# The second MLP's down projection: first products written by ScalarE, and the residual added by accumulating DMAs inside the stage

## The chip, the cores and the metric

The kernel runs on one core of one Trainium2 chip. It is one launch. The metric is the device time of that launch in microseconds (us), over several runs. All profile rows are of one profiled execution; times in them count from the start of its span.

The engines have short names. PE is the matrix engine (TensorE), PEld its weight loads, DVE the vector engine, ACT the scalar engine, POOL GpSimd. SP is the engine that issues nearly all DMAs here; "SPq" rows are those issues, and each of them only tells when the transfer was handed to the DMA engines, not when it landed.

## The reference, cut to what matters

The kernel computes one inference step of a two-layer encoder on 1056 rows, 1024 of a prompt and 32 of a sample, each of width 1024. Layer 0 is a matrix-memory mixer and an MLP, layer 1 a banded attention and an MLP. The change concerns layer 1's MLP:

```
u = x * (1 + sc2) + sh2
f = square(relu(u @ w_up[l])) @ w_down[l]
x = layer_norm(ALPHA * x + (1 + g2) * f, ln_g[l, 1], ln_b[l, 1])
```

w_up is 1024 x 4096 and w_down 4096 x 1024. g2 is a gate with one value per feature, and there are two sets of it: one for the prompt's rows, one for the sample's. The kernel works with the sum divided by ALPHA: x + gate * f, with gate = (1 + g2) / ALPHA. Everything is float32 in and out.

## The kernel before, in words

**Layout.** Activations lie with features on the 128 partitions: a tensor of width 1024 is 8 feature chunks (numbered fc) of 128 partitions x 1056 columns. The columns are cut into four quarters of 264 (QN); quarters 0 and 1 are column pair tp = 0, quarters 2 and 3 are tp = 1. The last quarter reaches from column 792 to 1055 and so holds both prompt and sample columns: whatever uses a gate there is two instructions, one of 232 columns and one of 32.

**Precision.** Each float32 operand is split in two parts: a high part, a cast by ACT (L89), and a low part, a subtraction by DVE (L90). A product is three matmuls: high x high, high x low, low x high. A weight is therefore of use to PE only when both ACT and DVE have handled it.

**Seven products.** Both projections of this MLP (function mlp7, L1140 and on) use a scheme with 7 products in place of 8 for a 2 x 2 block of blocks. The list PRODS (L1111) gives for each product the form of the weight, the form of the moving data, the PSUM bank it adds into, and the chunk and quarter of the result that take it. The products 0 and 2 share a bank, so do 3 and 5, and 4 and 6: the bank goes on accumulating, and it is read twice, once after each. So the second product of a bank can't start before the first reading of it has ended.

**The up stage.** PE computes 16 blocks of 256 hidden features (pb). Of each finished block, DVE and ACT make seven forms of the hidden values (h_forms: HL on L1189, HM on L1194), which SP stores to DRAM as hd. Blocks 14 and 15 are stored plainly (hpl, L1184).

**The down stage.** The hidden blocks 0 to 13 are worked off in five groups (GRP, L1108): group 0 has 2 blocks, groups 1 to 4 have 3 each. A unit is a group g and a number m from 0 to 3, the pair of feature chunks 2m and 2m + 1. For one unit PE runs the 7 products for both column pairs: 2 x 7 x 2 x 3 = 84 matmuls in group 0, 126 in the later ones (unit, L1437 and on; the matmul is on L1452). For each product the function L.add is called: in this kernel add_gated_at (L1077), in which DVE computes ACX = PSUM * gate + ACX in place (L1082). In each unit the product is added to one of four places, (chunk, quarter); products 0, 2, 3 and 6 are the first to reach their place, 1, 5 and 4 the second. Two PSUM banks of eight are to spare while one unit is at work. Unit (0, 0) is split by column pairs, tp = 1 first; the others take both pairs product by product.

**Order.** PE's order in the down stage is written out in the program (a manual schedule). The order on DVE, ACT, SP and POOL is made by the planner ahead of time, from its own estimate of when operands are ready; at run time each engine works in that order and waits only for the operands of the next instruction.

**The weights.** For each unit, forms (L1260 and on) loads two blocks of w_down (rdn_d, issued on L1265) into three raw buffers that are used in turn, and makes four tiles of weight forms (wf_d). The loads go out on SP, in the same queue as everything else.

**The moving data.** fill (L1426 and on) loads the hidden forms of the next products from hd into free buffers (fx, fx_e, fx_w; issued on L1133). In group 0 and at its end the data of group 1 are loaded.

**The residual.** ACX, the sums, is two tiles: chunks 0 to 3 and chunks 4 to 7. In the up stage the same memory holds transformed inputs (TF), so the residual x is stored to DRAM (xsp[2]) by the norm before, and comes back by reload (L2092): each call loads two chunks, 1056 KB, on SP (L2097), and makes the tile anew on the first of each half. Calls 0 and 1 stand in the up stage, once the transformed inputs of pair 1 are done with; call 2 at its end (up_end), call 3 at the first unit of the down stage. So the first add of each place finds the residual there.

After the five groups a plain block of the down projection follows (hpl, L118 to L120), and the norm and the output per row tile (norm_out), with which the kernel ends.

Layer 0's MLP runs through the same mlp7 without the seven products in its down stage (NW = 0), and reloads its residual there by the same calls.

Of the kernel before, what the change touches and what calls it, by code (L numbers as in the profile page):

```python
# [10 lines left out]
AF = mybir.ActivationFunctionType  # L11
ALU = mybir.AluOpType
# [21 lines left out]
def segs(t0, n):  # L34

    out = []
    if t0 < TP:
        m = min(t0 + n, TP) - t0
        out.append((0, m, 0))
        if m < n:  # L40
            out.append((m, n - m, 1))
    else:
        out.append((0, n, 1))
    return out
# [31 lines left out]
def trunk_kernel(ctx: ExitStack, tc: tile.TileContext, a, o):  # L76
    nc = tc.nc
# [62 lines left out]
    xsp = [dr.tile([P, KC, T], F32, name=f"xsp{l}") for l in range(4)]  # L140
# [26 lines left out]
    def ada_part(l, i):  # L167
        return ada[:, l * 48 + i * KC:l * 48 + (i + 1) * KC, :]
# [39 lines left out]
    tp = tpt("tp_c")  # L208
# [13 lines left out]
    tp = tpt("tp_p2")  # L222
# [694 lines left out]
    def make_layer(acc, pp, uo, cut=None):  # L917
# [159 lines left out]
        def add_gated_at(t0, n, ps, gate, fc):  # L1077

            for off, m, x in pieces(t0, n):
                for o, mm_, cnd in segs(t0 + off, m):  # L1080
                    xs = x[:, fc, o:o + mm_]
                    nc.vector.scalar_tensor_tensor(xs, ps[:, off + o:off + o + mm_], gate[:, fc, cnd:cnd + 1], xs,  # L1082
                                                   op0=ALU.mult, op1=ALU.add)

        def out_proj(groups, order, wsrc, mov, gate, after_tb, nm, width=None, after_pr=None):
            for gi, grp in enumerate(groups):
                ws = {pr: [wsrc(pr, half) for half in range(2)] for pr in grp}
                for ti in order:
                    n = TBS[ti][1]
                    nn = n if width is None else width[ti]  # L1090
                    for pr in grp:
                        for j in range(2):
                            ps = mm(f"op_{nm}_{2 * pr + j}_{ti}")
                            proj(ps[:, :nn], nn, ws[pr], j, lambda hl, k: mov(hl, k, ti))
                            add_gated(ti, ps, gate, 2 * pr + j)
                            flow.tick(n / 96)
                        if after_pr:
                            after_pr(ti, pr)
                    if gi == len(groups) - 1:
                        after_tb(ti)  # L1100

        return mm, norm, norm_out, out_proj, gain_shift, add_gated_at

    QN = T // 4
# [33 lines left out]
    def mlp7(L):  # L1140
# [5 lines left out]
        l, mm, NW = L.l, L.alloc, L.nw  # L1146
# [279 lines left out]
        def fill(g, into, most=99):  # L1426

            kg = GRP[g][1]
            while want and len(rooms.free) >= kg and most:
                most -= 1  # L1430
                if g >= len(GRP) - 3:
                    late = g == len(GRP) - 1 or g == len(GRP) - 2 and len(into) < 10
                    rooms.free.sort(key=lambda r: any(r[0] is t for t in f4s[:3]) == late)
                tp, f = want.pop(0)
                into[tp, f] = rooms.load(hd[g][tp][f], kg)

        def unit(g, m, phases, ws, step, after):  # L1437


            kg = GRP[g][1]  # L1440
            for tps in phases:
                ps = {}
                for i, (w, f, b, c, q) in enumerate(PRODS):
                    for tp in tps:
                        first = (tp, b) not in ps
                        if first:
                            ps[tp, b] = mm(f"dn{l}_{g}_{m}_{tp}_{b}")
                        p = ps[tp, b][:, :QN]
                        for k in range(kg):
                            t, s0 = fx[tp, f][k]  # L1450
                            for n_, (wl, xl) in enumerate(((0, 0), (0, 1), (1, 0))):
                                nc.tensor.matmul(p, ws[w][:, wl, k], t[:, s0, xl], start=first and k + n_ == 0,  # L1452
                                                 stop=k == kg - 1 and n_ == 2, skip_group_check=not first)
                        L.add((2 * tp + q) * QN, QN, p, L.gate, 2 * m + c)
                        after(tp, f)
                        flow.tick(QN * kg / 768)
                    if tps is phases[-1]:
                        step(i)
# [4 lines left out]
        def up_end():  # L1463
            if NW:
                for t in L.rooms(tp1):
                    rooms.add(t)
                fill(0, fx)
            L.reload(2 if NW else 1)
        lone = max(j for j, (_, tp) in enumerate(jobs) if tp == tp0)
        sevens = {}  # L1470
        first_h = [(c, hl) for c in range(4) for hl in range(2)]
# [1 line left out]
        with tc.manual_schedule(engines={mybir.EngineType.PE}):  # L1473
            for _, j, i in sorted((7 * j + 2 * i, j, i) for j in range(len(jobs)) for i in range(7)):
                n, tp = jobs[j]
                if i == 0:
                    sevens[j] = Seven(seq[n][0], tp, got[n])
                sevens[j].product(i, up_end if j == len(jobs) - 1 else None)
                if tp == seq[n][1][-1]:
                    advance(n, i)  # L1480
                if j == lone and i == 6 and NW:
                    rooms.add(ep.tile([P, KG, 2, QN], F32R, tag="e", name=f"fx_e{l}"))
                    for t in L.rooms(tp0):
                        rooms.add(t)
                if j > lone + 1:
                    if i in (2, 4, 6) and NW:
                        fill(0, fx, 1)
                    if i in (2, 5) and not NW and first_h:
                        h_load(0, *first_h.pop(0))
                    if i == 0 and NW and j < lone + 4:  # L1490
                        L.reload(j - lone - 2)
                    if i == 0 and not NW and j == lone + 5:
                        L.reload(0)
        nu = len(seq)
# [34 lines left out]
        with tc.manual_schedule(engines={mybir.EngineType.PE}):  # L1529
            for i, (g, m, phases) in enumerate(units):  # L1530
                more = g + 1 < len(GRP)
                if i == 0:
                    L.reload(3)
                if i == 0:
                    rooms.add(ring.tile([P, KG, 2, QN], F32R, tag="wc", name=f"fx_w{l}", bufs=6))
                    fill(0, fx)
                if m == 1 and more:
                    want += [(tp, f) for f in order_f for tp in L.pairs]
                if g and m == 2 and more:
                    fill(g + 1, nfx)  # L1540

                def after(tp, f):
                    if m == 3 and more:
                        rooms.free += fx[tp, f]
                        fill(g + 1, nfx)

                def step(j):
                    advance(nu + i, j)
                    if g == 0 and m in (1, 2):
                        fill(g + 1, nfx, 1)  # L1550
                unit(g, m, phases, got[nu + i], step, after)
                if m == 3:
                    assert not want
                    fx, nfx = nfx, {}
# [7 lines left out]
        for t0, n in L.blocks:  # L1562
            for fc in range(KC):
                ps = mm(f"dn{l}_{fc}_{t0}")
# [14 lines left out]
    acc = open_acc(acc_half0)  # L1579
# [1 line left out]
        acc_dma(xsp[0][:, :, t0:t0 + n], acc["all"].part(t0, n))  # L1581
    h_cm = tc.tile_pool(name="oapool", bufs=1, reuse_waits="tile")
    hp = h_cm.__enter__()
    mm, norm, _, out_proj, _, add_gated_at = make_layer(acc, bank, uap)
    combine(0, lng(0), lnb(0), ada_part(0, 4), ada_part(0, 3))
    norms = {}

# [35 lines left out]
    class L0:  # L1623
        wups = wup0
        l, nw, pace, alloc, add, gate = 0, 0, 480, mm, add_gated_at, ada_part(0, 5)
# [30 lines left out]
        def reload(m):  # L1656
            i = m // 2
            if m % 2 == 0:
                acc["all"].tiles[i] = acc_half0(i, "ACX")
            k = m % 2 * 2  # L1660
            nc.sync.dma_start(acc["all"].tiles[i][:, k:k + 2], xsp[3][:, 4 * i + k:4 * i + k + 2])
# [25 lines left out]
    for gi, grp in enumerate(((0, 1, 2), (3,))):  # L1687
        ws = {pr: [wblock(f"q{pr}_{half}", wq, 512 * half, 256 * pr) for half in range(2)] for pr in grp}
        for ti, (t0, n) in enumerate(TBS):
# [9 lines left out]
            for fc in [f for pr in grp for f in (2 * pr, 2 * pr + 1)]:  # L1699
                g, r = fc // 2, 2 * (fc % 2)  # L1700
                gp, e = g // 2, g % 2
                ps = mm(f"q_{fc}_{t0}")
                proj(ps[:, :n], n, ws[fc // 2], fc % 2, lambda hl, k: uap(hl, k, t0, n))
                for hd in range(2):
                    for off, m, cnd in segs(t0, n):
                        if cnd == 0:
                            dst = QOT[ti][:, e, gp, 0:m // 64, (r + hd) * 64:(r + hd + 1) * 64]
                            src = ps[64 * hd:64 * hd + 64, off:off + m].rearrange("p (c i) -> p c i", i=64)
# [312 lines left out]
    def acc_half(i, name):  # L2021
        return accp.tile([P, 4, T], F32, tag=f"acc{i}", name=f"{name}{i}")
# [13 lines left out]
    def u2ap(hl, k, t0, n):  # L2036
# [2 lines left out]
    open_u2(1)  # L2039
    psD_cm = tc.tile_pool(name="psD", bufs=1, space=PSUM, reuse_waits="tile")  # L2040
    psD = psD_cm.__enter__()
    mm, norm, norm_out, out_proj, gain_shift, add_gated_at = make_layer(
        acc, lambda name: psD.tile([P, 512], F32, tag="mm", name=name, bufs=8), u2ap, 2 * QN)

    def wo_get(pr, half):
# [25 lines left out]
    class L1:  # L2071
        wups = wup1
        l, nw, pace, alloc, add, gate = 1, 14, 64, mm, add_gated_at, ada_part(1, 5)
        blocks = [(0, 288), (288, 256), (544, 256), (800, 256)]
        pairs, quarters = (1, 0), (3, 2, 1, 0)
        first = FIRST
# [12 lines left out]
            t = accp.tile([P, 2, 2, KG, QN], F32R, tag=f"acc{i}", name=f"TF{i}")  # L2089
            return [[t[:, n, hl] for hl in range(2)] for n in range(2)]  # L2090

        def reload(m):  # L2092
            i = m // 2
            if m % 2 == 0:
                acc["all"].tiles[i] = acc_half(i, "ACX")
            k = m % 2 * 2
            nc.sync.dma_start(acc["all"].tiles[i][:, k:k + 2], xsp[2][:, 4 * i + k:4 * i + k + 2])  # L2097

        def rooms(pr):

# [66 lines left out]
```

## Time and profile before

| | us |
|---|---|
| Median of 3 runs | 2411.29 (2409.8 to 2412.41) |
| The profiled execution's own time | 2412.41 |
| Its span, first to last instruction | 2410.6 |
| PE busy in the span | 2342.7 (97%) |
| DVE busy | 1939.0 (80%) |
| ACT busy | 1206.0 (50%) |
| POOL busy | 168.1 (7%) |

How to read it. The span is cut by the profile in busy time per engine; "x" gives a number of instructions. A row of a timeline or a group gives line, engine, operation, and "out<-in" by the program's names. Behind a row, "[0.92 <-DVE ACX L1082]" means that the engine was idle for 0.92 us ahead of it, and that the instruction on DVE that wrote ACX on line 1082 ended this. The row of a group has its count, its total busy time, the mean of one in ns, and the idle time ahead of its instructions by what ended it. The mean granted clock of PE in this execution is 0.995.

A window's row gives busy time and instruction count of PE, PEld, DVE, ACT and POOL, then PE's granted clock as a share of full speed, the mean busy share of the 16 DMA engines (it is modelled and can pass 1), and the GB/s moved. Matmuls overlap, so in short stretches PE's busy time says less than the number of matmuls.

In the stretch that the change touches, the down stage of layer 1 starts around 2042 us, its five groups end near 2341 us, and the outputs end the kernel.

### The profile page before, as it was taken

What the parts mean: (1) busy time and instruction counts of PE and PEld (TensorE: products, weight loads), DVE (VectorE), ACT (ScalarE), POOL (GpSimd) and SP (SyncE); (2) the same over time, 40 slices, a digit from 0 to 9 for tenths busy, and PEclk for the clock granted to TensorE, in tenths of its full rate; (3) what the DMA queues carried; (4) which work ended last, traced back from release to release, by engine and by line L of the source; (5) the groups of instructions that cost most, each with busy time, mean ns of one, the idle gap of its engine ahead of it and who ended that gap; (6) DMA issues with size and microseconds to landing.
All of it is one profiled execution on the core that took longest, in us unless ns stands there. A gap on an engine that the chain in (4) does not pass through costs nothing. (4 is left out here: it accounts for less than half of the span.)

```text
span 2410.6 us, 44188 instructions
## 1 busy us (share of the span) xinstructions
PE 2342.7 (97%) x17180; PEld 2250.4 (93%) x17180; DVE 1939.0 (80%) x3903; ACT 1206.0 (50%) x2454; POOL 168.1 (7%) x320
## 2 busy tenths in 40 slices
PE   7999999999999999999999999999999999899997
PEld 4999999999999999999999987789999999899997
DVE  4888766778788789989888777756998889888778
ACT  4565557278666630101147467773776777222212
POOL 0111100000000000000000224420000000000003
PEclk9999999999999999999999999999999999999999
DMA  8343222526566896675512330051486779976642
GB/s 302 120 131 103 78 89 66 177 91 206 184 198 200 279 336 230 252 261 215 183 56 89 82 93 1 10 140 59 165 278 211 259 278 335 355 256 236 224 146 73
DMA packets 284277, 424.64 MB, mean 176 GB/s; under 512 B 15384, under 2 KB 205228, under 8 KB 278948
## 3 DMA queue, kind: packets, MB, share of 16 engines
q1 hardware_dynamic: 279860, 391.48, 48.3%
q10 hardware_dynamic: 4208, 30.35, 3.1%
q8 instruction: 135, 2.21, 0.4%
q14 instruction: 74, 0.61, 0.1%
HBM read 305.96 MB, written 118.17 MB: 176 GB/s over the span
## 5 line engine op out<-in xcount | busy, mean ns | idle before, releaser
L1082 DVE SCALAR_TENSOR_TENSOR ACX<-dn,ada,ACX 128x264 f32<-128x264 f32 (+6 forms) x664 | 281.8, 447 | 83.2 <-PE dn L1452 41.1
L1452 PE MATMUL dn<-fx,wf_d 128*128 128x264 f32 x2016 | 254.1, 285 | 6.8 <-DVE ACX L1082 3.5
L1452 PEld LDWEIGHTS dn<-fx,wf_d 128*128 128x128 f32 x2016 | 248.8, 188 | 9.0 <-DVE ACX L1082 3.0
L89 ACT CAST w_dn<-raw_dn 128x1024 fp32r<-128x1024 f32 x36 | 37.7, 1050 | 282.1 <-DVE aw L279 136.9
L118 PE MATMUL dn<-hs,w_dn 128*128 128x384 f32 (+2 forms) x512 | 161.2, 315 | 0.0
L119 PE MATMUL dn<-hs,w_dn 128*128 128x384 f32 (+2 forms) x512 | 161.0, 315 | 0.0
L120 PE MATMUL dn<-hs,w_dn 128*128 128x384 f32 (+2 forms) x512 | 156.4, 314 | 1.3 <-DVE w_dn L90 1.3
L1317 PE MATMUL up<-TF,wf_u 128*128 128x264 f32 x1056 | 143.2, 285 | 3.8 <-ACT H L1320 3.8
L1317 PE MATMUL up<-U,wf_u 128*128 128x264 f32 x1056 | 140.3, 285 | 1.7 <-ACT H L1320 1.2
L1317 PE MATMUL up<-u,wf_u 128*128 128x264 f32 x1056 | 139.7, 285 | 1.3 <-ACT wf_u L89 0.7
L279 DVE SCALAR_TENSOR_TENSOR aw<-radw,cs,aw 128x512 f32<-128x512 f32 x196 | 139.5, 743 | 1.1 <-DMA radw<-in_w_ada_dram 1.1
L1317 PEld LDWEIGHTS up<-TF,wf_u 128*128 128x128 f32 x1056 | 134.4, 189 | 4.8 <-ACT H L1320 4.6
L1317 PEld LDWEIGHTS up<-U,wf_u 128*128 128x128 f32 x1056 | 133.0, 188 | 3.0 <-ACT H L1320 1.6
L1317 PEld LDWEIGHTS up<-u,wf_u 128*128 128x128 f32 x1056 | 132.9, 188 | 1.9 <-ACT wf_u L89 0.9
L118 PE MATMUL dn<-U,w_dn 128*128 128x384 f32 (+2 forms) x416 | 129.4, 312 | 0.6 <-DVE ada L304 0.6
L119 PE MATMUL dn<-U,w_dn 128*128 128x384 f32 (+2 forms) x416 | 129.4, 312 | 0.0
L120 PE MATMUL dn<-U,w_dn 128*128 128x384 f32 (+2 forms) x416 | 125.9, 313 | 0.6 <-DVE w_dn L90 0.5
L1817 ACT ACTIVATE p<-p,mx 128x576 f32<-128x576 f32 (+9 forms) x132 | 86.6, 657 | 27.5 <-DVE mx L1814 25.2
L120 PEld LDWEIGHTS dn<-hs,w_dn 128*128 128x128 f32 x512 | 96.0, 188 | 2.0 <-DVE w_dn L90 1.8
L118 PEld LDWEIGHTS dn<-hs,w_dn 128*128 128x128 f32 x512 | 96.5, 189 | 0.1
L119 PEld LDWEIGHTS dn<-hs,w_dn 128*128 128x128 f32 x512 | 96.6, 189 | 0.0
L90 DVE TENSOR_TENSOR HL<-H,HL 128x1056 fp32r<-128x1056 f32 x64 | 80.3, 1254 | 20.0 <-ACT HL L89 19.9
(403 smaller groups left out, 7111.0 us busy)
## 6 DMA issues: line engine op xcount, KB each, us to landing
hpl<-HL SPq DMA_DIRECT2D x144, 264.0 KB
rdn_u<-in_w_up_dram SPq DMA_DIRECT2D x64, 512.0 KB
hd<-HL SPq DMA_DIRECT2D x28, 1056.0 KB
fx<-hd SPq DMA_DIRECT2D x50, 528.0 KB
radw<-in_w_ada_dram SPq DMA_DIRECT2D x24, 1024.0 KB
hd<-HM SPq DMA_DIRECT2D x28, 792.0 KB
raw_up<-in_w_up_dram SPq DMA_DIRECT2D x40, 512.0 KB
raw_dn<-in_w_down_dram SPq DMA_DIRECT2D x36, 512.0 KB
```

Of the source, the lines that this page charges most:

```text
L89: nc.scalar.copy(dst_h, src)
L90: (eng or nc.vector).tensor_sub(dst_l, src, dst_h.bitcast(F32))
L118: nc.tensor.matmul(ps, wh, mov(0, k), start=(k == 0), stop=False)
L119: nc.tensor.matmul(ps, wh, mov(1, k), start=False, stop=False)
L120: nc.tensor.matmul(ps, wl, mov(0, k), start=False, stop=(k == nk - 1))
L279: nc.vector.scalar_tensor_tensor(acc[cnd], raw[:, k], sc, acc[cnd], op0=ALU.mult, op1=ALU.add)
L1082: nc.vector.scalar_tensor_tensor(xs, ps[:, off + o:off + o + mm_], gate[:, fc, cnd:cnd + 1], xs, op0=ALU.mult, op1=ALU.add)
L1317: nc.tensor.matmul(p, self.ws[w][:, wl, k], moving(f, tp, xl, k), start=first and k + n_ == 0, stop=k == 3 and n_ == 2, skip_group_check=n ...
L1452: nc.tensor.matmul(p, ws[w][:, wl, k], t[:, s0, xl], start=first and k + n_ == 0, stop=k == kg - 1 and n_ == 2, skip_group_check=not first)
L1817: nc.scalar.activation(z, z, AF.Exp, bias=mx[:, 0:1], scale=-1.0, accum_out=mx[:, 1:2])
```

## The change

1. The reloads of layer 1 are gone. Only the tiles are made anew, by fresh, which issues nothing: half 0 after the up stage's work for pair 1 is done, half 1 at the end of the up stage.
2. In group 0 the products 0, 2, 3 and 6, the first to reach their place, call L.put in place of L.add. There ACT writes PSUM * gate into ACX, and reads no residual. The other three products add to that on DVE as before.
3. The residual is added by eight DMAs with an accumulate operation, one per chunk (528 KB), from xsp[2] in DRAM onto ACX. They are issued from POOL's queue. In the program's order they stand ahead of these units: (1, 1) for chunks 4 and 5, (1, 2) for chunks 6 and 7, (2, 1) for chunks 0 and 1, (2, 2) for chunks 2 and 3. A unit (g, m) adds to chunks 2m and 2m + 1.
4. Layer 0 keeps its reloads as they were.

The diff, cut to its core:

```diff
+        def put_gated_at(t0, n, ps, gate, fc):
+            for off, m, x in pieces(t0, n):
+                for o, mm_, cnd in segs(t0 + off, m):
+                    nc.scalar.activation(x[:, fc, o:o + mm_], ps[:, off + o:off + o + mm_], AF.Copy,
+                                         scale=gate[:, fc, cnd:cnd + 1])
+
+        def add_stored(fc, src):
+            nc.gpsimd.dma_start(acc["all"].tiles[fc // 4][:, fc % 4], src[:, fc], accum_op=ALU.add)
...
-                        L.add((2 * tp + q) * QN, QN, p, L.gate, 2 * m + c)
+                        put = L.put if g == 0 and i in (0, 2, 3, 6) else L.add
+                        put((2 * tp + q) * QN, QN, p, L.gate, 2 * m + c)
...
-            L.reload(2 if NW else 1)
+                L.fresh(1)
+            else:
+                L.reload(1)
...
-                    if i == 0 and NW and j < lone + 4:
-                        L.reload(j - lone - 2)
+                    if i == 0 and NW and j == lone + 2:
+                        L.fresh(0)
...
-                if i == 0:
-                    L.reload(3)
...
+                for m_ in {(1, 1): (2,), (1, 2): (3,), (2, 1): (0,), (2, 2): (1,)}.get((g, m), ()):
+                    for fc in (2 * m_, 2 * m_ + 1):
+                        L.stored(fc, xsp[2])
                 unit(g, m, phases, got[nu + i], step, after)
...
+        put, stored = put_gated_at, add_stored
...
-        def reload(m):
-            i = m // 2
-            if m % 2 == 0:
-                acc["all"].tiles[i] = acc_half(i, "ACX")
-            k = m % 2 * 2
-            nc.sync.dma_start(acc["all"].tiles[i][:, k:k + 2], xsp[2][:, 4 * i + k:4 * i + k + 2])
+        def fresh(i):
+            acc["all"].tiles[i] = acc_half(i, "ACX")
```

More of the change, by code (lines that the diff above doesn't have):

```diff
@@ L1100, in out_proj @@
                         after_tb(ti)
-        return mm, norm, norm_out, out_proj, gain_shift, add_gated_at
+        return mm, norm, norm_out, out_proj, gain_shift, add_gated_at, put_gated_at, add_stored
     QN = T // 4
@@ L1583, in trunk_kernel @@
     hp = h_cm.__enter__()
-    mm, norm, _, out_proj, _, add_gated_at = make_layer(acc, bank, uap)
+    mm, norm, _, out_proj, _, add_gated_at, _, _ = make_layer(acc, bank, uap)
     combine(0, lng(0), lnb(0), ada_part(0, 4), ada_part(0, 3))
@@ L2041, in trunk_kernel @@
     psD = psD_cm.__enter__()
-    mm, norm, norm_out, out_proj, gain_shift, add_gated_at = make_layer(
+    mm, norm, norm_out, out_proj, gain_shift, add_gated_at, put_gated_at, add_stored = make_layer(
         acc, lambda name: psD.tile([P, 512], F32, tag="mm", name=name, bufs=8), u2ap, 2 * QN)
```

## The prediction, made before the changed kernel ran

> **What bounds the kernel now.** I read the page first, then the chain of waits, then windows cut at the units of the second MLP's down projection, then the timelines of PE, of SP's DMA queue and of ACT there.
>
> The page:
>
> ```profile
> span 2410.6 us, 44188 instructions
> PE 2342.7 (97%) x17180; PEld 2250.4 (93%) x17180; DVE 1939.0 (80%) x3903; ACT 1206.0 (50%) x2454; POOL 168.1 (7%) x320
> ```
>
> PE is the bound of the whole, so the change can only give or take PE's idle time. The chain, in order of time (start, us, engine, tile, line), shows where that is:
>
> ```profile
> 1819.92 201.48 PE up L1317 x1656
> ...
> 2094.09 0.56 DVE wf_d L90
> 2094.70 4.40 PE dn L1452 x34
> 2099.10 0.73 issue
> 2099.83 241.67 PE dn L1452 x1980
> ```
>
> From 2099.83 the chain is PE alone for 241.67 us. Whatever the change does, if it only acts around group 0, can be read from the time of that row: it is my marker, and its shift goes to the end unchanged. The windows show how much there is to win:
>
> ```profile
> core 0: us, PE busy (x) PEld busy (x) DVE busy (x) ACT busy (x) POOL busy (x), PEclk, DMA share, GB/s
> 2042.50:2058.50 16.00, 13.34 (x98) 12.08 (x97) 15.36 (x37) 7.99 (x15) 0.00 (x0) 1.00 0.99 340
> 2058.50:2069.10 10.60, 10.43 (x87) 10.22 (x85) 7.91 (x21) 0.41 (x1) 0.00 (x0) 1.00 1.03 400
> 2069.10:2082.30 13.20, 11.08 (x85) 10.50 (x86) 12.76 (x37) 4.99 (x13) 0.00 (x0) 1.00 0.98 364
> 2082.30:2094.70 12.40, 10.92 (x89) 10.49 (x87) 9.42 (x24) 1.03 (x2) 0.00 (x0) 1.00 1.04 411
> ...
> 2172.00:2203.00 31.00, 31.00 (x257) 31.00 (x256) 25.62 (x61) 6.60 (x14) 0.00 (x0) 1.00 0.39 139
> ```
>
> Undisturbed (last row), 257 matmuls take 31.00 us, 0.121 us each. The first four windows are the four units of group 0 (m = 0 to 3, 84 matmuls each, 10.2 us at that pace). They take 16.0, 10.6, 13.2 and 12.4 us, with the DMA engines full (0.98 to 1.04). Later, PE has no gap. The same place on PE (start, us, tile; behind it the idle time and what ended it):
>
> ```profile
> 2057.72 0.97 PE L1452 MATMUL dn<-fx,wf_d 128*128 128x264 f32 x6 [0.75 <-DMA fx<-hd]
> 2058.53 0.89 PE L1452 MATMUL dn<-fx_e,wf_d 128*128 128x264 f32 x6
> ...
> 2073.70 4.62 PE L1452 MATMUL dn<-fx,wf_d 128*128 128x264 f32 x36 [0.92 <-DVE ACX L1082]
> 2079.28 3.16 PE L1452 MATMUL dn<-fx,wf_d 128*128 128x264 f32 x24 [0.96 <-DVE ACX L1082]
> 2082.28 0.89 PE L1452 MATMUL dn<-fx_e,wf_d 128*128 128x264 f32 x6
> ...
> 2089.22 4.66 PE L1452 MATMUL dn<-fx,wf_d 128*128 128x264 f32 x36 [0.68 <-DVE wf_d L90]
> ```
>
> fx_e heads a unit, so units 1 and 3 start at 2058.53 and 2082.28 (unit 2 at the window's edge, 2069.1). Unit 0 ends when its last fx has landed (2057.72), which is issued ahead of the reloads that go: 2058.53 stays. From there three units of 10.2 us and the first 36 matmuls of group 1 (4.4 us) would bring the marker to 2093.5 instead of 2099.83. **At most 6.3 us can be won**, 0.26%. (About 0.2%, 4.8 us, is what a measurement of this kernel can tell from no change.)
>
> **The change, part by part.**
>
> *The evictions.* What writes ACX from the start of group 0 to its end (the reloads on SP among it), and ACT's nearest operations, the copy out of PSUM and an activation with two scale and bias vectors:
>
> ```profile
> L1082 DVE SCALAR_TENSOR_TENSOR ACX<-dn,ada,ACX x72: 240/486/495, 2045.2 to 2093.7; 128x264 f32<-128x264 f32 x40, 128x232 f32<-128x232 f32 x16, 128x32 f32<-128x32 f32 x16
> L2097 SPq DMA_DIRECT2D ACX<-xsp x2: 550/644/739, 2050.1 to 2058.7; - x2
> ```
> ```profile
> L1320 ACT COPY H<-up 128x264 f32<-128x264 f32 x132 | 49.0, 371 | 13.5 <-PE up L1317 13.3
> ...
> L935 ACT ACTIVATE u<-ACC,comb 128x256 fp32r<-128x256 f32 x8 | 4.7, 591 | 2.3 <-DVE ACC L992 2.3
> ```
>
> Products 0, 2, 3 and 6 of four units and two column pairs go to ACT. Where a product reaches into the sample's columns it is two instructions, so 10 of a unit's 18 go, 40 of the 72. DVE loses about 40 x 0.43 = 17 us of this stretch (0.43 is the mean over 24 full ones, 8 of 232 columns and 8 of 32; the row spans 0.24 to 0.49). A put costs between 0.37 and 0.59 us; I take 0.45, near the copy, since it has one vector: 40 x 0.45 = 18 us on ACT, 4.5 a unit, beside at most 5.0 us that ACT has in units 1 to 3. That is hidden. What it buys on PE is the two waits for adds in unit 2 (0.92, 0.96), the wait at 2089.22 (0.68; the weights' subtraction stood in DVE's queue between adds) and, of the start of group 1, the time that the subtraction at 2094.09 stood behind adds. Together some 3.5 us, if nothing else is late.
>
> *The reloads.* SP's queue (start, us, line, tile) and the casts of weights on ACT that answer to it:
>
> ```profile
> 2063.57 8.02 SPq L1265 DMA_DIRECT2D rdn_d<-in_w_down_dram  x2
> ...
> 2080.75 2.35 SPq L1265 DMA_DIRECT2D rdn_d<-in_w_down_dram  x2
> ```
> ```profile
> 2068.63 0.41 ACT L89 CAST wf_d<-rdn_d 128x256 fp32r<-128x256 f32 x1 [11.49 <-DMA rdn_d<-in_w_down_dram]
> ...
> 2092.53 0.51 ACT L89 CAST wf_d<-rdn_d 128x384 fp32r<-128x384 f32 x1 [0.50 <-DMA rdn_d<-in_w_down_dram]
> ```
> ```profile
> L2097 SPq DMA_DIRECT2D ACX<-xsp x4: 550/670/992, 1977.4 to 2058.7; - x4
> ```
> ```profile
> ACX<-xsp SPq DMA_DIRECT2D x8, 1056.0 KB
> ```
> ```profile
> 2045.00:2105.00 60.00, 52.84 (x407) 50.19 (x407) 51.61 (x132) 15.31 (x34) 0.00 (x0) 1.00 1.00 376
> ```
>
> The weights that SP asks for at 2080.75 are those of group 1's first unit, and the cast at 2092.53, ended by their landing some 10 us later, is **the gate**: PE gets them at 2094.70. The full DMA queue sets it. All four reloads are issued from 1977.4 to 2058.7, 1056 KB each; the two at 2050.1 and 2058.7 stand in front of the gate: 2 x 1056 KB at 376 GB/s is 5.75 us of a queue that is never empty. Without them the first cast of unit 2 (2068.63) comes about 5 us earlier, before unit 1 ends, so what unit 2 waits for at 2069.1 goes too. Of the 5.75 us up to 1.7 can be lost where SP stands 8.02 us for a free buffer (2063.57) while the queue drains. So the gate would be at 2086.8 to 2088.5. The two earlier ones I cost at nothing: the chain's first row is PE alone from 1819.92 on for 201.48 us, with no wait for a DMA; if that cover were gone it would be a gain of at most as much again. SP's own issue time (0.6 us each) hides nothing now.
>
> *The accumulating DMAs.* In the program they stand ahead of units of groups 1 and 2, but POOL has nothing else here (0.00 in every window). Each is held back by its operands alone, and nothing is queued behind it. So for rows 4 and 5 they start when unit 2's adds are done, by my count at about 2079 and not at 2111; for rows 6 and 7 after unit 3, at about 2089; for rows 0 to 3 after the first two units of group 2, near 2173 and 2188, where the DMA share is 0.39 and nothing suffers. The adds that wait for them come three units (46 us) later, so no wait on DVE.
>
> The first pair falls into the full queue, ahead of the gate. Its bytes are one reload's, 1056 KB, 2.9 us of the DMA engines if an accumulate costs what a load does. No row shows an accumulate, nor how two queues share full engines. Below: it takes only what is left over, the gate stays at 2086.8. Above: it goes first at two or three times the price, 8.6 us and more. I take the load's price, the nearest row, and equal turns: it starts at 2080 to 2081 and has all of its 2.9 us before the gate's data land, so the gate is at 2089.7 to 2091.4, middle 2090.6.
>
> The Trainium skill, "DMA: Bandwidth & Descriptors", section "Queues, rings and completion order", says that an engine takes turns between queues packet by packet, which is the equal turns taken here; no run shows it yet.
>
> *The sum.* The gate moves from 2092.53 to 2090.6: -1.9 us. Behind the gate PE now starts 2.2 us later; with DVE freed (0.51 for the cast, 0.55 for the subtraction) 1.3 us, so -0.9 more. The second pair, in the queue from 2089, takes another 2.9 us from the inputs of group 1's first unit and the next weights; their slack behind the gate covers most of it, and I charge 1.1. Sum: -1.9 - 0.9 + 1.1 = **-1.7 us**. Of the 6.3 us the gate and the second pair keep 4.6. The profiled execution took 2412.41 us, 1.8 over its span, and the median of the runs is 2411.29; laid on the median this gives **2409.6**.
>
> **The rivals.**
>
> *The accumulates don't touch the gate* (they start later than I say, held until the whole half of the sums is written, or they get only idle engines). For it: a wait by whole tiles would put all four behind unit 3. Against it: the queue has no idle time until 2105. Gate at 2086.8 to 2088.5, PE gets through group 0 without waits, marker at 2093.5 to 2095: -5.5 us, 2405.8.
>
> *An accumulate costs twice a load.* It reads its destination as well as its source. Pair one has 5.75 us to take, but by turns no more than the queue itself moves from 2081 to the gate's data, 3.5 to 5 us: gate at about 2092.0. -0.5 there, -0.9 from DVE, and pair two at twice its 1.1: +0.8, 2412.1. The Trainium skill, "Collectives: The Full Stack", section "The bandwidth ceiling: the fold count and why AG ≠ RS ≠ AR", gives two source reads as the reason why an adding transfer runs at about half the rate of a copy.
>
> *The accumulates slow the queue all through group 1's first unit* (the side of slower). The queue, full until 2105 in the window above, comes some 5 us earlier without the reloads, so from 2081 on it has about 16 us of work left for that unit (my estimate: what stood in it from 2086 to 2102). Equal turns with both pairs all that time make it 32. Against the 16 more stand the 5 us of the earlier start and about 5 us by which the last inputs land ahead of their use: +6, 2417.3. It decides when the four take over 16 us of the engines, that is 2.8 times a load's price.
>
> *The puts stand behind casts that wait for weights* (ACT's queue is in order). At 2068.63 ACT waited 11.49 us for a DMA; a put behind such a cast keeps a PSUM bank and so the fifth product. In unit 3 this would add the rest of the unit, 36 matmuls, behind the gate instead of ahead of it: +2.7 on the sum, 2412.3. Against it: DVE's adds, under the same planner, mostly stand ahead of the weights' work.
>
> *The change does nothing* (the adds were hidden and the DMA bytes only move by 30 us): within the first two cases, 0.
>
> **How the numbers follow.** Forecast 0.36, double price 0.22, no touch on the gate 0.22, slow queue 0.14, puts behind casts 0.06. Faster by over 0.2% is the third, and a little of the forecast where the gate comes early: 0.24. Slower by over 0.2% is the slow queue and a little of the last: 0.16. Within: 0.60. The likeliest case gives 2409.6, with its own bounds -4.5 to +1. The range runs from the full 6.3 us won (2405.0) to +4.2 (2415.5); outside it lies most of the slow queue and little else.
>
> **What would show it.** In the profile after: the put lines on ACT x40 at about 0.45 us; 40 fewer adds on DVE in group 0; SP without L2097's rows; unit 2 without waits for adds; the cast behind group 1's first weights at about 2090.6; POOL's DMA issues near 2079, 2089, 2173 and 2188; the long PE row starting near 2098. I am wrong if the gate comes before 2088 or after 2094, if the issues come only at their place in the program, if PE waits for a put, or if a gap opens on PE after group 1's first unit.

## The result, and the profile after

The changed kernel took **2419.01 us** in the median of 6 runs (2417.5 to 2420.32), the kernel before 2410.55 in 6 runs beside it (2406.25 to 2412.81): ratio 1.0038, 95% interval 1.0025 to 1.005. It is slower, by some 8 us, and outside the range. The profiled execution took 2418.34 us. Of its page, the span, the engines and two DMA queues (packets, MB, share of 16 engines' span):

```profile
span 2416.6 us, 44207 instructions
...
PE 2342.4 (97%) x17180; PEld 2250.9 (93%) x17180; DVE 1920.2 (79%) x3863; ACT 1221.6 (51%) x2494; POOL 175.1 (7%) x328
...
q1 hardware_dynamic: 279284, 387.15, 47.8%
...
q0 software_dynamic: 1152, 4.33, 0.9%
```

PE is busy as long as before (2342.7), so the page shows the loss as idle time; the rows below put some 2 us of it down to a lower clock. DVE has the 40 fewer instructions, ACT the 40 more. q0 is POOL's queue, and its 4.33 MB are the eight accumulates. They cost 0.9/4.33 of the engines per MB, q1's transfers 47.8/387.15: 1.7 times as much.

The chain of waits (start, us, what) no longer ends in one row of PE from the start of group 1 on:

```profile
2115.87 50.71 PE dn L1463 x414
...
2170.03 9.88 DMA rdn_d<-in_w_down_dram
...
2181.03 5.87 PE dn L1463 x45
...
2188.09 9.35 DMA rdn_d<-in_w_down_dram
2198.50 0.93 DVE wf_d L90 x2
...
2200.10 147.03 PE dn L1463 x1188
```

PE alone from 2115.87, then twice a load of weights that takes almost 10 us, both in group 2, where the prediction had no wait at all. PE's timeline there (idle time and what ended it in brackets), and DVE's rows for the first difference that it forms from new weights:

```profile
2167.14 1.63 PE L1463 MATMUL dn<-fx_w,wf_d 128*128 128x264 f32 x12
...
2181.03 4.39 PE L1463 MATMUL dn<-fx,wf_d 128*128 128x264 f32 x33 [2.38 <-DVE ACX L1082]
2185.25 1.63 PE L1463 MATMUL dn<-fx_w,wf_d 128*128 128x264 f32 x12
...
2200.10 7.26 PE L1463 MATMUL dn<-fx,wf_d 128*128 128x264 f32 x42 [4.45 <-DVE ACX L1082]
2207.21 1.62 PE L1463 MATMUL dn<-fx_w,wf_d 128*128 128x264 f32 x12
```
```profile
2180.01 0.56 DVE L1292 TENSOR_TENSOR s_d<-rdn_d,rdn_d 128x384 f32<-128x384 f32 x1 [4.67 <-DMA rdn_d<-in_w_down_dram]
...
2197.53 0.56 DVE L1292 TENSOR_TENSOR s_d<-rdn_d,rdn_d 128x384 f32<-128x384 f32 x1 [6.85 <-DMA rdn_d<-in_w_down_dram]
```

In the kernel before, the first of these (L1281 there) had no wait and the second had 0.80 us:

```profile
2179.03 0.55 DVE L1281 TENSOR_TENSOR s_d<-rdn_d,rdn_d 128x384 f32<-128x384 f32 x1
...
2192.52 0.56 DVE L1281 TENSOR_TENSOR s_d<-rdn_d,rdn_d 128x384 f32<-128x384 f32 x1 [0.80 <-DMA rdn_d<-in_w_down_dram]
```

PE waits for adds (L1082), because DVE, whose order is fixed, stands at L1292 in front of those adds until weights land. The issues on POOL and on SP say what met there:

```profile
...
2085.46 0.86 POOL L1094 DMA_DIRECT2D ACX<-xsp  x1 [7.92 <-DVE ACX L1082]
2088.27 0.89 POOL L1094 DMA_DIRECT2D ACX<-xsp  x1 [1.95 <-ACT ACX L1089]
2167.46 0.88 POOL L1094 DMA_DIRECT2D ACX<-xsp  x1 [78.30 <-DVE ACX L1082]
2169.89 0.86 POOL L1094 DMA_DIRECT2D ACX<-xsp  x1 [1.56 <-DVE ACX L1082]
2186.44 0.86 POOL L1094 DMA_DIRECT2D ACX<-xsp  x1 [15.69 <-DVE ACX L1082]
2187.82 0.88 POOL L1094 DMA_DIRECT2D ACX<-xsp  x1 [0.52 <-DVE ACX L1082]
```
```profile
2167.80 0.38 SPq L1276 DMA_DIRECT2D rdn_d<-in_w_down_dram  x1
...
2170.03 0.38 SPq L1276 DMA_DIRECT2D rdn_d<-in_w_down_dram  x1
...
2186.58 1.89 SPq L1276 DMA_DIRECT2D rdn_d<-in_w_down_dram  x2
```

The end of a unit releases both: its last adds set the accumulates free, and its last weight forms set the raw weight buffers free. So accumulates are issued at 2167.46 and 2169.89 and weights at 2167.80 and 2170.03, and again all four within some 2 us from 2186.44 on. The windows behind the second meeting (columns as in the prediction):

```profile
2190.00:2195.00 5.00, 5.00 (x43) 5.00 (x42) 0.49 (x1) 0.93 (x2) 0.00 (x0) 1.00 1.04 220
2195.00:2200.00 5.00, 0.65 (x6) 0.44 (x4) 2.46 (x7) 0.92 (x2) 0.00 (x0) 0.76 0.37 95
2200.00:2205.00 5.00, 4.90 (x24) 4.93 (x25) 4.64 (x12) 0.00 (x0) 0.00 (x0) 0.56 0.00 0
```

The DMA engines are full (1.04) and move 220 GB/s, where they moved 340 to 411 in the full windows of before; DVE works 0.49 of 5 us. After PE's gap the granted clock is 0.76 and then 0.56, so PE's 42 matmuls take 7.26 us instead of 5.08 (0.121 each).

**Where the time went.** In PE's timeline there is one fx_w row in each of the eight units of groups 1 and 2, the next one in the first unit of group 4, and an exu row late in the up stage, where both kernels are still alike. From these rows follow the lengths of nine pieces, and each less the same of before is a loss that doesn't depend on what came earlier in the execution. Before they are, from 2008.10 (exu) and 2104.30 (the first fx_w) on, 96.20, 15.37, 15.41, 15.35, 20.48, 15.36, 15.36, 15.36 and 65.81 us. The first piece holds the end of up and group 0; the next three steps lie in group 1, the one from 4 to 5 reaches into group 2, the next three lie there, and the last piece covers group 3.

| kernel | to 1st fx_w | 1 to 2 | 2 to 3 | 3 to 4 | 4 to 5 | 5 to 6 | 6 to 7 | 7 to 8 | 8 to 9 | sum |
|---|---|---|---|---|---|---|---|---|---|---|
| the change | -3.43 | 2.88 | 0.03 | 0.00 | 0.00 | 2.75 | 6.60 | 0.01 | 0.04 | +8.88 |
| no accumulates | -2.26 | 0.00 | 0.02 | 0.28 | 0.07 | 0.00 | 0.00 | 0.00 | 0.00 | -1.89 |
| chunks 4 to 7 only | -3.20 | 2.87 | 0.01 | 0.00 | 0.00 | 0.00 | 0.00 | 0.00 | 0.00 | -0.32 |
| chunks 0 to 3 only | -4.98 | 0.00 | 0.00 | 0.00 | 0.00 | 2.99 | 6.17 | 0.01 | 0.01 | +4.20 |
| plain loads | -2.94 | 0.00 | 0.00 | 0.00 | 0.02 | 0.00 | 1.85 | 0.00 | 0.00 | -1.07 |
| quarters | -4.12 | 2.14 | 0.00 | 0.25 | 0.07 | 0.00 | 0.53 | 0.01 | 0.00 | -1.12 |
| one chunk to a unit | -4.29 | 0.00 | 2.25 | 2.88 | 0.07 | 0.89 | 4.32 | 0.01 | 4.19 | +10.32 |
| the same in quarters | -3.06 | -0.01 | 0.18 | 0.63 | 0.08 | 0.00 | 0.55 | 0.00 | 1.06 | -0.57 |
| copies, two chunks | -3.03 | -0.01 | 0.00 | 5.25 | 2.39 | 5.56 | 6.33 | -0.01 | -0.07 | +16.41 |
| copies, one chunk | -5.07 | -0.01 | 2.39 | 2.20 | 0.05 | 1.31 | 6.15 | -0.02 | 2.08 | +9.08 |
| held, two chunks | -4.57 | -0.01 | 0.01 | 0.51 | 0.05 | 9.61 | -0.01 | -0.01 | -0.08 | +5.50 |
| held, one chunk | -3.81 | -0.01 | 0.22 | 0.24 | 0.06 | 1.86 | -0.01 | -0.02 | 1.84 | +0.37 |
| held, apart | -4.46 | 0.00 | 0.00 | 0.23 | 0.06 | 1.50 | 1.00 | -0.01 | -0.07 | -1.75 |

The first row sums to +8.88, beside +8.46 between the medians: 0.55 won around group 0 and its end (the first two columns, below called the seam), 9.35 lost in group 2. The other rows belong to the experiments below; each is one profiled execution, so a first column may differ by a microsecond or two by chance.

### The profile page after: what moved, and what is told of

Same layout as the page of the kernel before. It is cut to its first block, busy times and chain, and to the rows that moved or that the text cites. A ratio compares the mean times of both kernels' runs of the same rounds, so it can differ in the third digit from the quotient of the medians.

```text
span 2416.6 us, 44207 instructions
## 1 busy us (share of the span) xinstructions
PE 2342.4 (97%) x17180; PEld 2250.9 (93%) x17180; DVE 1920.2 (79%) x3863; ACT 1221.6 (51%) x2494; POOL 175.1 (7%) x328
## 3 DMA queue, kind: packets, MB, share of 16 engines
q1 hardware_dynamic: 279284, 387.15, 47.8%
q0 software_dynamic: 1152, 4.33, 0.9%
## 5 line engine op out<-in xcount | busy, mean ns | idle before, releaser
L1082 DVE SCALAR_TENSOR_TENSOR ACX<-dn,ada,ACX 128x264 f32<-128x264 f32 (+6 forms) x624 | 264.5, 447 | 85.8 <-PE dn L1463 44.3
```

## The experiments

The theory: an accumulate keeps the DMA engines about twice as long as a load of the same size, a pair of them is released at about the same moment as the next unit's weights, the weights land late, DVE stands, PE runs out of PSUM banks. The rivals: what ACT now does, or the missing reloads, cost the time; the loss sits in the full queue of group 1's first unit, as the prediction's slow case has it; POOL's queue costs it, whatever it carries.

### Which accumulates

The first run leaves all accumulates out, the second those of chunks 0 to 3, the third those of 4 to 7.

```diff
-{(1, 1): (2,), (1, 2): (3,), (2, 1): (0,), (2, 2): (1,)}
+{}                          # first
+{(1, 1): (2,), (1, 2): (3,)}   # second
+{(2, 1): (0,), (2, 2): (1,)}   # third
```

> The eight accumulating DMAs are left out, so the residual x is missing from the MLP's sums. Theory (the accumulates hold up the weight loads rdn_d of group 2, whose rows are small): the two gaps of 2.4 and 4.5 us on PE in group 2 are gone and with them 9.4 us; group 0 and its seam lose the accumulates' share too, so the time falls below before, 2405 to 2409.5 us. Rival A (ACT's puts or the planner's new order cost the time): still above 2414.

Measured: 2403.78 us, before 2408.07 (this and the next three runs): ratio 0.9982, interval 0.9973 to 0.9991. This is a little below the 2405 us expected. Puts and missing reloads by themselves make the kernel faster; they are not the cause.

> Only the accumulates of chunks 4 to 7 stay (in the seam after group 0); the residual of chunks 0 to 3 is left out. Theory: group 2 runs without a gap over 1 us; 2408.5 to 2411.5 us. Rival B (an accumulate costs its bytes wherever it lies): half of the loss stays, 2414 to 2415.5.

Measured: 2409.23 us, 1.0004 (0.9996 to 1.0013). Only the 2.87 us of group 1's first step are there, as in the change.

> Only the accumulates of chunks 0 to 3 stay (group 2); the residual of chunks 4 to 7 is left out. Theory: group 2 keeps its two gaps and loses 8 to 10 us against before, the seam gains 1 to 4: 2414 to 2419 us. Rival B: half of the loss, 2414 to 2415.5, with group 2's loss near 4.

Measured: 2413.67 us, 1.0025 (1.0015 to 1.0035), a little under what was expected, since the seam gains more without its own accumulates (-4.98, and no loss behind it). Group 2 loses 9.17 as in the change. So the loss is in group 2 and belongs to the accumulates of chunks 0 to 3, not to the full queue.

### The accumulate, or POOL's queue

```diff
-nc.gpsimd.dma_start(x, src[:, fc], accum_op=ALU.add)
+nc.gpsimd.dma_start(x, src[:, fc])
```

> All eight DMAs stay on POOL's queue, but without the accumulate operation: they overwrite the sums with the residual, so the products of the first units are lost. Theory (what counts is how long a row of the other queue holds an engine): a plain row takes half an accumulate's time, the weight loads are held up by half, group 2 loses 1 to 4 us in place of 9.4: 2408 to 2413 us. Rival C (POOL's queue itself, its descriptors or its quarrel with DVE for memory): as after, 2417 to 2420.

Measured: 2406.59 us, 0.9998 (0.9988 to 1.0008), a little below the 2408 us expected. The same bytes at the same places in the same queue lose 1.87 us in group 2 instead of 9.35. Of its page and of DVE's timeline:

```profile
q0 software_dynamic: 1152, 4.33, 0.5%
```
```profile
2180.31 0.56 DVE L1292 TENSOR_TENSOR s_d<-rdn_d,rdn_d 128x384 f32<-128x384 f32 x1 [1.67 <-DMA rdn_d<-in_w_down_dram]
...
2195.25 0.56 DVE L1292 TENSOR_TENSOR s_d<-rdn_d,rdn_d 128x384 f32<-128x384 f32 x1 [4.00 <-DMA rdn_d<-in_w_down_dram]
```

The same packets take 0.5% of the engines instead of 0.9%. The trace's packet records give 336 ns for a row of 4224 bytes that is accumulated and 164 ns for one that is loaded. A chunk has 128 rows, 8 for each of 16 engines: a pair of chunks keeps the engines 16 x 0.336 = 5.4 us, as plain loads 2.6 us. DVE's waits of 4.67 and 6.85 are 1.67 and 4.00 here, some 3 us shorter each, which is the difference of the two. So the cause is not POOL's queue whatever it carries.

The packet records also show how two queues share an engine. For the change, accumulate rows and other rows that began in each half microsecond (count, KB, median ns of one), first beside rows of moving data (fx_e), then beside rows of weights:

```
2175.5  POOL's queue: 16, 68 KB, 336 ns   SP's queue: 16, 68 KB, 178 ns
2176.0  POOL's queue: 16, 68 KB, 336 ns   SP's queue: 16, 68 KB, 178 ns
2194.5  POOL's queue: 21, 89 KB, 336 ns   SP's queue: 23, 24 KB, 60 ns
2195.0  POOL's queue: 22, 93 KB, 336 ns   SP's queue: 22, 23 KB, 60 ns
```

One row for one row, whatever their lengths; and nearly every loaded row there takes 14 ns longer than one that moves alone (178 for 164 ns, 60 for 46). A weight row has 1 KB, so beside accumulates weights move at 24 KB in half a microsecond, some 48 GB/s. (From 2191 to 2192.5 no weight row moved at all, though the second load had been issued at 2188.09; the records don't say why.) The turns alone don't set the delay: the last accumulate row starts at 2196.18 and the last weight row at 2197.07, so the weights are whole only when the pair's 5.4 us of engine time are over. The Trainium skill, "DMA: Bandwidth & Descriptors", section "Queues, rings and completion order", has an engine take turns between queues by packets of typically 9 to 17 descriptors; that it takes turns agrees, but here, by these counts, one turn is one row.

### Shorter rows

Each chunk's accumulate becomes four of 264 columns, first in the change's four units, then with the chunks spread over eight units (below).

```diff
-nc.gpsimd.dma_start(x, src[:, fc], accum_op=ALU.add)
+for t in range(0, T, QN):
+    nc.gpsimd.dma_start(x[:, t:t + QN], src[:, fc, t:t + QN], accum_op=ALU.add)
```

> The changed kernel with each chunk's accumulating DMA cut into four of 264 columns: the same bytes at the same place, but rows of 1056 bytes in place of 4224. Taking turns row by row: the weights' rows of 1024 bytes get a turn after a quarter of the time, so their first load lands after some 4 to 6 us instead of 10, group 2 loses 2 to 6 us instead of the 9.4, and the median is 2412 to 2416 us. If only the engines' time for the accumulates' bytes counts, or POOL's issues: group 2 loses the same 9 us or more (16 more issues there), 2417 to 2421 us.

Measured: 2408.52 us, before 2408.49 (this and the next two): 0.9998 (0.9989 to 1.0007). Group 2 loses 0.53, less than expected, and the reason isn't the one that was expected alone. POOL's first issues there:

```profile
2154.03 0.86 POOL L1095 DMA_DIRECT2D ACX<-xsp  x1 [49.27 <-DMA fx<-hd]
2155.13 0.86 POOL L1095 DMA_DIRECT2D ACX<-xsp  x1 [0.23 <-issue]
2161.18 2.68 POOL L1095 DMA_DIRECT2D ACX<-xsp  x3 [5.18 <-DVE ACX L1082]
2166.37 2.68 POOL L1095 DMA_DIRECT2D ACX<-xsp  x3 [2.52 <-DVE ACX L1082]
```

A quarter waits for its own columns' adds alone, so the eight issues of the first pair lie between 2154.03 and about 2169, five of them ahead of the first request for weights (2164.25). The run doesn't tell shorter turns from an earlier, wider spread. An estimate from the row times speaks for the spread: a unit's weights are 768 rows, 48 for each engine. Turn by turn beside a pair of whole chunks they take 16 x (336 + 60) + 32 x 46 ns = 7.8 us, beside quarters 48 x (104 + 60) ns = 7.9 us, no less. The run does exclude the engines' time as such, wherever it falls, which is more here than the change's 0.9%, with less lost:

```profile
q0 software_dynamic: 4608, 4.33, 1.2%
```

### One chunk to a unit

```diff
-for m_ in {(1, 1): (2,), (1, 2): (3,), (2, 1): (0,), (2, 2): (1,)}.get((g, m), ()):
-    for fc in (2 * m_, 2 * m_ + 1):
-        L.stored(fc, xsp[2])
+for fc in {(1, 1): (0,), (1, 2): (2,), (1, 3): (4,), (2, 0): (6,),
+           (2, 1): (1,), (2, 2): (3,), (2, 3): (5,), (3, 0): (7,)}.get((g, m), ()):
+    L.stored(fc, xsp[2])
```

> The changed kernel with the eight accumulating DMAs one to a unit (chunks 0, 2, 4, 6, 1, 3, 5, 7 behind the units from group 1's first to group 2's last) in place of two to a unit in four units; the group 0 stage then has none. Taking turns: the seam keeps its gain of about 4 us, as it did with rows 0 to 3 alone, and a single chunk holds a weight load up by at most some 3 us, which the order of DVE's work forgives in most units: 2404 to 2408 us, below the kernel before. If a single accumulate is enough to make DVE wait for weights: each of eight units loses 1 to 3 us, 2411 to 2420 us.

Measured: 2417.33 us, 1.0039 (1.0025 to 1.0052). The seam keeps -4.29, but single chunks lose up to 4.32 each, the last one 4.19 in group 3: half a pair is not harmless, against the theory's number (2404 to 2408). A whole chunk still is released only by a unit's last adds, as the weights are.

> One chunk to a unit as in the run before, and each in four DMAs of 264 columns. Taking turns: the weight loads are held up by 1 us or less, so no unit waits: 2403 to 2407 us, as fast as or a little faster than whole chunks. If bytes or issues alone count: the same as whole chunks or slower by up to 3 us.

Measured: 2406.66 us, 0.9996 (0.9987 to 1.0004). The same chunks in the same units cost 2.5 us from the first fx_w row on instead of 14.6.

### Moving only the moment

If it is the meeting that costs, whole accumulates must be free once they are issued behind the weights. The first two tries put a copy out of the two new weight tiles ahead of each accumulate:

```diff
+# in step(3) of a unit, ahead of its accumulates
+for n_, r in enumerate(raws.pop(f"d{l}_{i + 2}")):
+    nc.gpsimd.tensor_copy(held[:1, n_:n_ + 1], r[:1, 0, :1])
+L.stored(fc, xsp[2])
```

> Whole-row accumulating DMAs as in the change, but each pair is held until the next weights have landed: in the third product of a unit GpSimd first copies one number out of each of the two weight tiles just asked for, and only then issues the accumulates. Chunks 0 to 3 stay in the same two units of group 2 as in the change; 4 to 7 go to the last unit of group 1 and the first of group 2. The bytes and the issues are the same as in the change. If it is the weight load's turns that cost: four units, none of which loses more than 1 us, the weights' difference on VectorE no longer waits for a DMA, and with the seam free of accumulates the median is 2403 to 2407 us. If it is the accumulates' own time on the engines, or the adds that wait for them: four units lose 4 to 7 us each as in the change's group 2, 2412 to 2425 us.

> One chunk to a unit as in the run with whole chunks spread over eight units (2417.3 us), and each held until the next weights have landed, as in the run beside this one. Turns: none of the eight units loses more than 0.5 us, 2402 to 2406 us. If a single accumulate costs by its own engine time or its adds: 2415 us or more, as without the hold.

Measured: 2421.94 us, before 2407.39: 1.0055 (1.0041 to 1.007); and 2418.84, 1.0051 (1.0038 to 1.0064). Nothing was held. POOL in the first of them, in the order in which it ran:

```profile
2156.44 0.86 POOL L1095 DMA_DIRECT2D ACX<-xsp  x1 [10.21 <-DVE ACX L1083]
2158.70 0.89 POOL L1095 DMA_DIRECT2D ACX<-xsp  x1 [1.41 <-DVE ACX L1083]
2170.86 0.17 POOL L1569 COPY held<-rdn_d 1x1 f32<-1x1 f32 x1 [11.27 <-DMA rdn_d<-in_w_down_dram]
```

No data ties an accumulate to the copy, and the planner set the accumulates ahead of it. So the edit didn't do what it says, and the two runs say nothing on a hold. They do repeat the loss: four pairs in groups 1 and 2 lose 19.5 us, the two pairs in the change's group 2 lose 9.4.

The next runs tie them by data: a number of each new weight tile, times zero, is added to the chunk's first column.

```diff
+nc.gpsimd.tensor_mul(z, raw[0][:, 0, :1], raw[1][:, 0, :1])
+nc.gpsimd.tensor_scalar(z, z, 0.0, 0.0, op0=ALU.mult, op1=ALU.mult)
+nc.gpsimd.tensor_add(x[:, :1], x[:, :1], z)
 nc.gpsimd.dma_start(x, src[:, fc], accum_op=ALU.add)
```

> As the run with the hold, where GpSimd issued the accumulates ahead of the copies that were to hold them. Now the hold is in the data: the product of one number of each weight tile just asked for, times zero, is added to the first column of the chunk before its accumulate, so the accumulate can't be issued before those weights have landed. Same places (four units of two chunks), same bytes. If it is the weight load's turns that cost: the weights land in about 3 us, VectorE's difference doesn't wait for a DMA, the four units lose at most 1 us each in place of the 5 us each of that run, and the median is 2403 to 2407 us. If it is the accumulates' own time on the engines or the adds that wait for them: 2412 us or more, four units still losing 4 to 6 us each.

> The same hold through the data, one chunk to a unit in eight units. Turns: no unit loses more than 0.5 us, 2402 to 2406 us, below the kernel before. Own time or adds: 2412 us or more, as without the hold (2417.3 us).

Measured: 2412.34 us, before 2408.38: 1.0017 (1.0008 to 1.0026); and 2408.95, 1.0006 (0.9997 to 1.0014). Both are slower than expected. The first median by itself would fit the rival too (2412 or more); the units tell the two apart, since the rival has all four lose 4 to 6 us. One unit shows why the time is long. POOL, SP and DVE there:

```profile
2165.49 0.89 POOL L1100 DMA_DIRECT2D ACX<-xsp  x1 [0.30 <-POOL ACX L1099]
...
2167.75 0.92 POOL L1100 DMA_DIRECT2D ACX<-xsp  x1 [0.36 <-POOL ACX L1099]
...
2180.57 0.90 POOL L1100 DMA_DIRECT2D ACX<-xsp  x1 [0.36 <-POOL ACX L1099]
```
```profile
2165.16 0.38 SPq L1283 DMA_DIRECT2D rdn_d<-in_w_down_dram  x1
...
2167.42 0.38 SPq L1283 DMA_DIRECT2D rdn_d<-in_w_down_dram  x1
...
2186.69 2.60 SPq L1283 DMA_DIRECT2D rdn_d<-in_w_down_dram  x2
```
```profile
2178.73 0.56 DVE L1300 TENSOR_TENSOR s_d<-rdn_d,rdn_d 128x384 f32<-128x384 f32 x1 [7.38 <-DMA rdn_d<-in_w_down_dram]
...
2192.78 0.56 DVE L1300 TENSOR_TENSOR s_d<-rdn_d,rdn_d 128x384 f32<-128x384 f32 x1 [1.29 <-DMA rdn_d<-in_w_down_dram]
```

In this unit the weights that held the pair had landed late themselves, so the pair met the load after them: accumulates at 2165.49 and 2167.75, weights at 2165.16 and 2167.42. DVE waited 7.38 us and the step lost 9.61. The next pair, issued at 2180.57 behind the weights that had landed by 2178.73, met no load of weights (the next is asked for at 2186.69), and the steps behind it lost nothing (-0.01 each). Of four like pairs, the three that met no load of weights lost 0.51 us and twice nothing, the one that did 9.61. That is the theory's sharpest test, within one execution; the one pair also differs in standing in the first unit of a group.

The last run takes pairs out of the first units of groups, where this happened. There the same step then loses 1.50 us instead of 9.61:

```diff
+{(1, 2): (2, 3), (1, 3): (4, 5), (2, 1): (0, 1), (2, 2): (6, 7)}   # held
```

> The hold through the data again, two chunks to a unit, but none in the first unit of a group: there the next weights are asked for late and in two steps, and the accumulates of the run before fell together with them (9.6 us lost in that one unit, 0.6 us at most in each of the other three). Chunks 2 and 3 in group 1's third unit, 4 and 5 in its fourth, 0 and 1 in group 2's second, 6 and 7 in its third. Turns: each of the four units loses at most 0.6 us, the seam's gain of 4 to 5 us stays, and the median is 2403 to 2406 us, below the kernel before and as fast as the run without accumulates. If accumulates cost by their own time: 2412 us as in the run with that hold, or more.

Measured: 2406.06 us, before 2407.93: 0.9992 (0.9983 to 1.0001). The eight accumulates now lose 2.8 us in groups 1 and 2, and the seam keeps -4.46. It is clearly faster than the change; that it is faster than the kernel before isn't shown, since the interval takes in 1. One step lost 1.50, more than the 0.6 expected.

## Why the prediction was wrong

The step that failed is the one on rows 0 to 3: accumulates "near 2173 and 2188, where the DMA share is 0.39 and nothing suffers". The times were about right (2167.46 and 2186.44 in an execution that was 3.25 us early). The price was not: it cost 2.75 + 6.60 = 9.35 us. A share of 0.39 is a mean over 31 us. In 5 us windows of the kernel before it is 0.79 and 1.03 from 2172 on, and 0.49 from 2187 on, around the two requests for weights; and the end of a unit releases weights and accumulates together. Of the first loss PE's wait is 2.38; the granted clock is 1.00 there, and no row explains the other 0.37. The second is 4.45 of waiting and 7.26 - 5.08 = 2.2 of clock. The part's "nothing is queued behind it" looked at POOL's queue alone, and not at what another queue asks of the same engines at that moment. The run with chunks 0 to 3 alone shows the place, the one with plain loads the price, the held runs the meeting.

Point by point, with 3.25 us taken off forecast times for the earlier start of this execution (exu at 2004.85 for 2008.10):

*Evictions.* Forecast 0.45 us a put, 40 of them, hidden. The groups of ACT in the stage:

```profile
L1089 ACT ACTIVATE ACX<-dn,ada 128x264 f32<-128x264 f32 x24 | 11.4, 481 | 10.5 <-PE dn L1463 10.2
...
L1089 ACT ACTIVATE ACX<-dn,ada 128x232 f32<-128x232 f32 x8 | 3.6, 456 | 5.1 <-PE dn L1463 5.0
...
L1089 ACT ACTIVATE ACX<-dn,ada 128x32 f32<-128x32 f32 x8 | 2.3, 284 | 0.0
```

17.3 us over 40 is 0.43: right. Unit 2 has no waits for adds any more, but unit 1 has one of 1.10 us. Hidden it was not wholly: the waits of PE hold 1.8 us for puts, both in unit 0 (1.22 and 0.61), one of the signs named as against me.

*The gate.* Forecast 2090.6, so 2087.3 here; the cast came at 2086.66. The marker, forecast near 2098 (2094.8), came at 2093.15, behind an idle time put down to issue as before. To this point the change wins 3.4 us, where -1.9 - 0.9 = -2.8 was forecast. That the gate came so near is in part luck: the first pair's rows took twice the price assumed, and unit 0, which was to stay as it was, ended 1.4 us sooner (unit 1 starts at 2053.86, where 2058.53 less 3.25 was forecast).

```profile
2086.66 0.51 ACT L89 CAST wf_d<-rdn_d 128x384 fp32r<-128x384 f32 x1 [4.29 <-DMA rdn_d<-in_w_down_dram]
...
2101.94 0.51 ACT L89 CAST wf_d<-rdn_d 128x384 fp32r<-128x384 f32 x1 [10.68 <-DMA rdn_d<-in_w_down_dram]
```
```profile
2093.15 4.64 PE L1463 MATMUL dn<-fx,wf_d 128*128 128x264 f32 x36 [0.92 <-issue]
```

*The second pair.* Charged 1.1, it cost 2.88: the next weights, asked for at 2088.45 beside the accumulates of 2085.46 and 2088.27, were cast at 2101.94. PE's waits in and behind group 1's first unit (the longest 0.84) are the gap that was named as a sign of error, the rival of the slow queue in mechanism and half its price (+6). The seam comes to -0.55 instead of -1.7.

*The rivals.* That an accumulate costs twice a load was right as a price (336 against 164 ns), as the Trainium skill, "Collectives: The Full Stack", section "The bandwidth ceiling: the fold count and why AG ≠ RS ≠ AR", has it for two reads (no run here shows that a second read is the reason); it was priced around group 0 only, and I took the load's price for the forecast. No rival had a wait in group 2. Puts behind casts did not decide: all of unit 3 ran ahead of the gate, where PE waited 1.13 us. One sentence of the text ahead is wrong: products 0, 2, 4 and 6 share one bank, 3 and 5 another; the four that are put are still the first at their places.

What stays open: how much of the quarters' gain is shorter turns and how much their earlier release, for which only the estimate speaks, and the 1.86 and 1.84 us that held single chunks still lose at the changes to groups 2 and 3.

## What to carry to other kernels

A low mean share of the engines does not make a DMA free: look up what else is issued within some microseconds of it, and who waits for that. Two transfers that the same point of the program releases, as the end of a unit here, meet each time; tie the one that has time to the landing of the other, through data, or cut it so that its parts are released earlier. An accumulating DMA took twice a load's time on the engines here; count it so until a run shows otherwise.

## What the runs showed of the hardware

- A row of 4224 bytes takes 336 ns when it is accumulated, 164 ns when it is loaded; one of 1056 bytes 104 ns accumulated.
- Beside accumulates, the other queue moved one row for each accumulated row, so that rows of 1 KB beside accumulates of 4 KB moved at some 48 GB/s.
- After a PE gap of 4.45 us the granted clock stood at 0.76 and 0.56 in two windows of 5 us, and 42 matmuls took 2.2 us more: the wait of 4.45 us cost 6.6.
